# Eight of 22 gated tiles of a down projection as seven block products in place of eight

## The chip, the cores and the metric

One core of a Trainium2 chip runs the kernel. Its engines work side by side, each on a queue of its own that it takes strictly in order: TensorE (PE; PEld is its weight load) multiplies into PSUM, VectorE (DVE) and ScalarE (ACT) do elementwise work, GpSimd (POOL) does some too and issues DMAs, SyncE (SP) only issues DMAs. An instruction that has to wait for another engine or a DMA holds up all that stands behind it on its engine. The metric is the device time of one execution in microseconds (us).

## The reference

A trunk of two layers on a sequence of 1040 positions (16 learned ones and 1024 of input) and 1024 features. Each layer has an attention half, which the change leaves alone, and a feed-forward half:

```python
def conv_ffn(x, w_up, conv_w, conv_b, w_down):
    h = x @ w_up                                  # 1024 -> 2 * 2816
    hc = conv_b + sum(shifted(h, j) * conv_w[j] for j in range(3))
    u, g = jnp.split(hc, 2, axis=-1)
    return (jax.nn.silu(g) * u) @ w_down          # 2816 -> 1024
...
    h = h + conv_ffn(rms_norm(h, ffn_norm[i]), w_up[i], ...)
```

2816 gated features are 22 tiles of 128. The last operation, `@ w_down` and the sum to the residual `h`, is what is changed. All is float32.

## The kernel before, in words

Features lie on the 128 partitions and positions along the free dimension, so that a tile is 128 x 1040 (128 x 1024 in the last layer's down projection, which drops the learned positions). A float32 product is made of three faster ones: each operand is split in a high part, rounded to the type `float32r`, and a low part, the rest. `split` and `weights` do that with a cast on ScalarE (`hi`) and a subtraction on VectorE (`lo`), and `mm3` issues the three matmuls hi·hi, lo·hi, hi·lo (lines 216 to 218).

The up projection (`ffn_up`) makes, for each of the 22 tiles `j`, the two output tiles u and g of 128 features. It does the pair as a 2 x 2 block product with seven block products in place of eight (the scheme of Strassen in Winograd's form): the outputs u and g are the two block rows, the 1024 input features are halved into the inner blocks, and the positions into the two block columns (`HALVES`). Sums of weight blocks (`up_operand`) and of input halves are formed ahead, the seven products p = 1 to 7 are 4 x 2 x 3 matmuls of 260 or 258 columns each, and `evacuate` adds the results out of PSUM. After the last product of a tile, a convolution on ScalarE and VectorE, the gate and a store of the gated tile to DRAM (`actd`) follow. VectorE, ScalarE and the DMA queues are ordered by a planner at build time; TensorE keeps the order of the program.

The down projection then takes the 22 gated tiles in five groups (`FGROUPS`: 5, 5, 5, 4 and 3). `load_act` loads a gated tile (SyncE) and splits it (ScalarE `ah`, VectorE `al`). Within a group and for each of the eight output tiles `m`, `dense3` runs over the group's gated tiles and the chunks of positions (400, 384 and 256 columns in layer 0, 512 and 512 in layer 1), and VectorE adds the sums to the residual tile `hT[m]`, which is in SBUF all that time: it was stored to DRAM (`hm`) in the first half of the layer and is loaded back at the beginning of the down projection. `stream` fetches and splits the weights of one output tile ahead. While the last up tile's seven products run, `during_last` loads ten gated tiles as slots come free; when a group ends its slots take the group after the next. The last three gated tiles (`down_last`) go chunk by chunk, with their weights in slots, so that the next layer's norm can follow.

Buffers: 33 slots of one 128 x 1040 tile, and 6 more in the FFN, are handed out by `Slots.get` and returned by `put`; whoever gets a slot waits for the last reader of its last content. Four 2-bank places of PSUM serve the up projection; the down projection opens a pool of eight single banks.

Of the kernel before, what the change touches and what calls it, by code (L numbers as in the profile page):

```python
# [32 lines left out]
CH_DOWN = [(16, 512), (528, 512)]  # L33
CTILES = [(0, 4), (4, 7), (7, 9)]
FT, NT, FIRST = 116, 9, 112
CH_FOX = [(0, 344), (344, 348), (692, 348)]
# [8 lines left out]
NV = 203  # L45
V_FIN = DEPTH * NV

FGROUPS = [(0, 5), (5, 5), (10, 5), (15, 4), (19, 3)]
HALVES, HALVES_LAST = (0, 520, 520), (8, 524, 516)
AHEAD = 4  # L50
NSPLIT = 4

# [80 lines left out]
class Kern:  # L133
# [843 lines left out]


    def up_operand(self, lyr, j, p, fw, raws, odd):
        nc = self.nc  # L980
        if j == 2 and p in (1, 2):
            src = fw.tile([128, 4, 128], F32, tag="raw2", name="raw2")
            nc.sync.dma_start(src[:], self.wm[lyr, M_UP + 4][:, 4 * p - 4:4 * p, :])
            return self.up_split(src, fw, odd)
        if j not in raws:
            u, g = self.wm[lyr, M_UP + 2 * j], self.wm[lyr, M_UP + 2 * j + 1]
            q = raws[j] = {}
            for name, src, k0, own in (("A11", u, 0, True), ("A21", g, 0, False), ("A22", g, 4, False), ("A12", u, 4, True)):
                q[name] = self.wp.tile([128, 4, 128], F32, tag="raw", name="raw", bufs=4) if own else \
                    fw.tile([128, 4, 128], F32, tag="raw2", name="raw2")  # L990
                nc.sync.dma_start(q[name][:], src[:, k0:k0 + 4, :])
        q = raws[j]

        def combine(out, a, b, op):
            if out not in q:
                q[out] = fw.tile([128, 4, 128], F32, tag="raw2", name="raw2")
            nc.vector.tensor_tensor(out=q[out][:], in0=q[a][:], in1=q[b][:], op=op)
# [8 lines left out]
        return self.up_split(src, fw, odd)  # L1006

    def up_split(self, src, fw, odd):
# [4 lines left out]
        nc.scalar.copy(hi[:], src[:])  # L1013
        nc.vector.tensor_tensor(out=lo[:], in0=src[:], in1=hi[:].bitcast(F32), op=ALU.subtract)  # L1014
        return [(hi[:, k, :], lo[:, k, :]) for k in range(4)]

    def ffn_up(self, lyr, mix, hT, pp, fw, halves, o0, during_last):
        nc, s = self.nc, self.slots
# [218 lines left out]
        s.put(t)  # L1237
        acts[j] = (ah, al)

    def down_tiles(self, lyr, hT, pp, o0, dchunks, acts):  # L1240
        nc, s = self.nc, self.slots

        def down(i, m):
            g0, ng = FGROUPS[i]

            def f(w):
                def ev(ps, c0, n):
                    h = hT[m][:, c0:c0 + n]
                    nc.vector.tensor_tensor(out=h, in0=ps, in1=h, op=ALU.add)
                self.dense3(pp, w, [acts[j] for j in range(g0, g0 + ng)], dchunks, ev)  # L1250
                if m == KD - 1:
                    for j in range(g0, g0 + ng):
                        s.put(*acts.pop(j))
                    if i + 2 < len(FGROUPS):
                        a, b = FGROUPS[i + 2]
                        for j in range(a, a + b):
                            self.load_act(j, o0, acts)
            return (self.wd[lyr, m][:, g0:g0 + ng, :], f)
        return [down(i, m) for i in range(len(FGROUPS) - 1) for m in range(KD)]

    def down_last(self, lyr, hT, pp, dchunks, acts, at_end, es):

        nc, s = self.nc, self.slots
        g0, ng = FGROUPS[-1]
        w, held = [], []
        for m in range(KD):
            if m % 2 == 0:
                pair = [s.get(F32R, "wl", (128, 2, 4, 128), es) for _ in range(2)]
                held += pair
            w.append(self.weights(self.wd[lyr, m][:, g0:g0 + ng, :], [x[:, m % 2, :, :] for x in pair]))  # L1270
        nxt = at_end()
        a = [acts[j] for j in range(g0, g0 + ng)]
        for c0, n in dchunks:
            for m in range(KD):
                ps = pp.tile([128, 512], F32, tag="mm", name="mm")
                for k in range(ng):
                    self.mm3(ps[:, :n], w[m][k], a[k], c0, n, k == 0, k == ng - 1)
                h = hT[m][:, c0:c0 + n]
                nc.vector.tensor_tensor(out=h, in0=ps[:, :n], in1=h, op=ALU.add)
                final = nxt["gain"] is None  # L1280
                if final and c0 + n == T and m >= KD // 2:

                    sq = nxt["tp"].tile([128, 256], F32, tag="sql", name="sql", bufs=4)[:, :n]
                    nc.scalar.activation(sq, h, AF.Square)
                    nxt.setdefault("late", []).append(sq)
                else:
                    self.norm_feed(nxt, m, h, c0, n, nc.vector if final and c0 + n == T else None)
                if not final:
                    nc.sync.dma_start(self.hd[m][:, c0:c0 + n], h)
                elif m == 5 and c0 != dchunks[0][0]:  # L1290
                    self.norm_scale(nxt, pp, *before)
                    if c0 + n < T:
                        self.final(nxt, hT, pp, *before, pool=4)
            if final and c0 + n == T:
                nxt["parts"] = nxt.pop("late")
                self.norm_scale(nxt, pp, c0, n)
                self.final(nxt, hT, pp, *before, pool=KD + 1)
                self.final(nxt, hT, pp, c0, n, pool=KD + 1)
            before = (c0, n)
        for x in a:  # L1300
            s.put(*x)
        s.put(*held)
        return nxt
# [19 lines left out]
    def run(self):  # L1323
# [17 lines left out]
        for lyr in range(DEPTH):  # L1341
# [5 lines left out]
            acts, early = {}, {1: 2, 6: 2, 2: 1, 7: 2, 5: 1, 4: 1, 3: 1}  # L1347

            def during_last(p):
                for _ in range(early[p]):  # L1350
                    self.load_act(len(acts), o0, acts)
            with tc.tile_pool(name=f"ffn{lyr}", bufs=1, reuse_waits="tile") as fp, \
                    tc.manual_schedule(engines={mybir.EngineType.PE}):
                ids = s.add(fp, 6, f"e{lyr}_")
                with tc.tile_pool(name=f"ups{lyr}", bufs=1, space=PSUM, reuse_waits="tile") as pp, \
                        tc.tile_pool(name=f"up{lyr}", bufs=7, reuse_waits="tile") as fw:
                    self.ffn_up(lyr, mix, hT, pp, fw, HALVES_LAST if last else HALVES, o0, during_last)
                with tc.tile_pool(name=f"dps{lyr}", bufs=8, space=PSUM, reuse_waits="tile") as pp, \
                        tc.tile_pool(name=f"down{lyr}", bufs=1, reuse_waits="tile") as dp:
                    ids += s.add(dp, 3 if last else 4, f"d{lyr}_")  # L1360
                    hT = [s.get(F32, f"h{k}", first=ids) for k in range(KD)]
                    for k in range(KD):
                        nc.sync.dma_start(hT[k][:, o0:T], self.hm[k][:, o0:T])
# [9 lines left out]
                    self.stream(self.down_tiles(lyr, hT, pp, o0, CH_DOWN if last else CH, acts))  # L1373
# [60 lines left out]
```

## Time and profile before

| | us |
|---|---|
| median of three runs | 2647.05 (2646.37 to 2649.61) |
| profiled execution | 2645.09 |
| its span, first to last instruction | 2643.3 |
| first four groups of the down projection, layer 0 | 1071.8 to 1288.9 of the span |
| the same, layer 1 | 2380.2 to 2591.5 |

A line of a group reads: line, engine, operation, out<-in, shape, xcount | busy us, mean ns of one | idle time ahead of them and what ended it. A line of the timeline reads: start, duration in us, engine, line, operation, out<-in, shape, xcount, and in brackets the idle time before it and its releaser. The duration of an instruction overlaps a little with the next on the same engine, so that the distance of two starts is its price in a row. A stretch reads: start:end, length, and for each engine its busy us and instruction count, then the granted share of TensorE's clock, the DMA engines' busy share and GB/s.

### The profile page before, as it was taken

How to read it: one execution, taken by the hardware profiler on the slowest of the kernel's cores; microseconds unless marked ns; L12 is line 12 of the kernel's file. 1: busy time of each engine (PE TensorE's matmuls, PEld its weight loads, DVE VectorE, ACT ScalarE, POOL GpSimd, SP SyncE). 2: the span in 40 equal slices, each digit the busy share in tenths (PEclk: the TensorE clock that was granted, in tenths of full speed). 3: DMA queues.
4: the chain of work that ended last, by engine and by line, in shares of the span. 5: the costliest groups of instructions: out<-in, count | busy, mean ns of one | idle time of the engine just before them, and what ended most of it. 6: DMA issues, size and time to landing. Idle time of an engine off the chain costs nothing.

```text
span 2643.3 us, 46336 instructions
## 1 busy us (share of the span) xinstructions
PE 2523.9 (95%) x18102; PEld 2407.2 (91%) x18102; DVE 1759.9 (67%) x3484; ACT 1240.1 (47%) x2677; POOL 457.9 (17%) x596
## 2 busy tenths in 40 slices
PE   8999999897999999999999999998989999999997
PEld 7988898897999999999999888887889999998886
DVE  7655676759877777643665666666698767776335
ACT  6345665645544445421343565665455444453112
POOL 4033333333000000000201333332320000000002
PEclk9999999998999999999999999999999999999999
DMA  3222124341222222632312222142512222245222
GB/s 125 65 83 70 47 83 124 106 131 58 97 81 76 85 77 92 217 94 58 103 56 65 75 72 74 56 138 91 158 51 85 83 81 77 83 139 189 65 55 77
DMA packets 114476, 240.72 MB, mean 91 GB/s; under 512 B 14432, under 2 KB 36192, under 8 KB 114256
## 3 DMA queue, kind: packets, MB, share of 16 engines
q1 hardware_dynamic: 96000, 182.27, 22.7%
q0 software_dynamic: 16384, 53.18, 5.5%
q8 instruction: 142, 2.33, 0.4%
q10 hardware_dynamic: 1872, 2.31, 0.2%
q14 instruction: 78, 0.64, 0.1%
HBM read 174.01 MB, written 50.91 MB: 85 GB/s over the span
## 4 chain that ended last, share of the span: by engine, by line
PE 77%; DVE 13%; ACT 4%; issue 3%; DMA 2%; POOL 2%; DVEq 0%; SPq 0%; POOLq 0%; ACTq 0%
PE mm L216 12%; PE mm L217 12%; PE mm L218 12%; PE up L216 10%; PE up L217 10%; PE up L218 10%; PE av L706 2%; PE tr L688 2%; DVE S L655 1%; DVE x L1038 1%; PE wo L217 1%; PE wo L216 1%; PE wo L218 1%; DVE PT L331 1%; ACT P L667 1%
## 5 line engine op out<-in xcount | busy, mean ns | idle before, releaser
L216 PE MATMUL up<-x,hi 128*128 128x260 f32 (+1 forms) x2464 | 701.3, 285 | 22.7 <-DVE hu L1180 20.3
L217 PE MATMUL up<-x,lo 128*128 128x260 f32 (+1 forms) x2464 | 699.2, 284 | 0.0
L218 PE MATMUL up<-x,hi 128*128 128x260 f32 (+1 forms) x2464 | 698.5, 283 | 0.0
L216 PEld LDWEIGHTS up<-x,hi 128*128 128x128 f32 x2464 | 467.5, 190 | 24.4 <-DVE hu L1180 20.7
L217 PEld LDWEIGHTS up<-x,lo 128*128 128x128 f32 x2464 | 467.9, 190 | 0.1
L218 PEld LDWEIGHTS up<-x,hi 128*128 128x128 f32 x2464 | 467.8, 190 | 0.0
L216 PE MATMUL mm<-xh,hi 128*128 128x348 f32 (+4 forms) x1056 | 365.1, 346 | 0.0
L218 PE MATMUL mm<-xl,hi 128*128 128x348 f32 (+4 forms) x1056 | 340.9, 323 | 0.0
L217 PE MATMUL mm<-xh,lo 128*128 128x348 f32 (+4 forms) x1056 | 340.8, 323 | 0.0
L1014 DVE TENSOR_TENSOR lo<-raw,hi 128x512 fp32r<-128x512 f32 x308 | 212.9, 694 | 146.2 <-ACT hi L1013 146.2
L183 ACT CAST hi<-raw 128x512 fp32r<-128x512 f32 (+1 forms) x264 | 142.3, 543 | 329.8 <-PE mm L218 240.0
L217 PE MATMUL mm<-ah,lo 128*128 128x400 f32 (+1 forms) x760 | 266.4, 351 | 0.2 <-DVE lo L185 0.2
L218 PE MATMUL mm<-al,hi 128*128 128x400 f32 (+1 forms) x760 | 265.9, 350 | 0.0
L216 PE MATMUL mm<-ah,hi 128*128 128x400 f32 (+1 forms) x760 | 265.8, 350 | 0.0
L185 DVE TENSOR_TENSOR lo<-raw,hi 128x512 fp32r<-128x512 f32 (+1 forms) x196 | 120.7, 620 | 181.1 <-ACT hi L183 177.5
L1013 ACT CAST hi<-raw 128x512 fp32r<-128x512 f32 x308 | 190.3, 620 | 107.6 <-PE up L218 92.7
L216 PEld LDWEIGHTS mm<-xh,hi 128*128 128x128 f32 x1056 | 201.0, 190 | 6.0 <-issue 5.3
L217 PEld LDWEIGHTS mm<-xh,lo 128*128 128x128 f32 x1056 | 200.9, 190 | 0.4 <-issue 0.3
L218 PEld LDWEIGHTS mm<-xl,hi 128*128 128x128 f32 x1056 | 199.9, 189 | 0.4 <-issue 0.3
L1203 POOL DMA_DIRECT2D actd<-cv x44 | 23.4, 533 | 830.0 <-DVE cv L1202 830.0
L667 ACT ACTIVATE P<-S,m 116x460 f32<-116x460 f32 (+2 forms) x224 | 124.8, 561 | 76.9 <-DVE m L655 72.6
L331 DVE TENSOR_TENSOR PT<-tr,PT 116x464 fp32r<-116x464 f32 (+3 forms) x240 | 122.1, 516 | 55.8 <-ACT PT L330 54.1
(248 smaller groups left out, 5269.0 us busy)
## 6 DMA issues: line engine op xcount, KB each, us to landing
raw<-in_wm_dram SPq DMA_DIRECT2D x328, 256.0 KB, 2.6
raw<-in_wd_dram SPq DMA_DIRECT2D x64, 256.0 KB, 2.6
actd<-cv POOLq DMA_DIRECT2D x22, 520.0 KB, 2.9
st<-actd SPq DMA_DIRECT2D x22, 520.0 KB, 4.9
actd<-cv POOLq DMA_DIRECT2D x22, 512.0 KB, 3.0
st<-actd SPq DMA_DIRECT2D x22, 512.0 KB, 4.8
cb<-cd SPq DMA_DIRECT2D x16, 520.0 KB, 4.2
kA<-kA SPq DMA_DIRECT2D x24, 260.0 KB, 3.8
```

The costliest lines, as they stand in the source:

```text
L183: nc.scalar.copy(hi[:, :n, :], raw[:, :n, :])
L185: eng.tensor_tensor(out=lo[:, :n, :], in0=raw[:, :n, :], in1=hi[:, :n, :].bitcast(F32), op=ALU.subtract)
L216: nc.tensor.matmul(ps, wh, xh[:, c0:c0 + n], start=first, stop=False, skip_group_check=more)
L217: nc.tensor.matmul(ps, wl, xh[:, c0:c0 + n], start=False, stop=False, skip_group_check=more)
L218: nc.tensor.matmul(ps, wh, xl[:, c0:c0 + n], start=False, stop=last, skip_group_check=more)
L331: nc.vector.tensor_tensor(out=lo, in0=src, in1=hi.bitcast(F32), op=ALU.subtract)
L655: nc.vector.tensor_tensor_reduce(out=S[:rows, :n], in0=S[:rows, :n], in1=cb[:rows, c0:k1], scale=1.0, scalar=(BIG if ci == 0 else m[:rows, ...
L667: nc.scalar.activation(P[:rows, :n], S[:rows, :n], AF.Exp, scale=-1.0, bias=m[:rows, nch - 1:nch], accum_out=(den if nch == 1 else d3[:row ...
L688: nc.tensor.transpose(tr[:w, j, :rows], P[:rows, o:o + w], id_)
L706: nc.tensor.matmul(av[:, a:width], w.rearrange("p a b -> p (a b)"), x, start=(t == 0 and i == 0), stop=(t == last and i == 1))
L1013: nc.scalar.copy(hi[:], src[:])
L1014: nc.vector.tensor_tensor(out=lo[:], in0=src[:], in1=hi[:].bitcast(F32), op=ALU.subtract)
```

## The change

The groups are now one plain group of three gated tiles whose sums leave SBUF ("n"), one block group of eight ("s"), two plain groups of four whose sums are added to the residual in SBUF ("r"), and the last three as before. In the block group a pair of output tiles is the two block rows, the eight gated tiles are two inner halves of four, and the positions the two block columns: seven block products for a pair in place of eight, with weight sums made by the same function as in the up projection (`block_operand`, split off `up_operand`).

The operands of the block group, seven sums or differences of gated tiles, each split in hi and lo, are made by the new generator `prepare`. It yields how many slots its next step needs, and `pump` lets it go on when so many are free: after each product of the last up tile, after each plain tile and after each block product. Sums of the plain "n" group and of the block group are copied or added out of PSUM into a slot and added to the residual in DRAM (`hm`) by DMAs that accumulate, eight for each of the two groups and layer, on the GpSimd queue. Only then is the residual loaded (`load_residual`). All plain tiles work on the two halves of positions in two pieces, so on 260 or 256 columns, and use the four 2-bank places of the up projection, in whose pools the stage now runs.

```diff
-FGROUPS = [(0, 5), (5, 5), (10, 5), (15, 4), (19, 3)]
+GROUPS, LAST = (("n", 0, 3), ("s", 3, 8), ("r", 11, 4), ("r", 15, 4)), (19, 3)
+HALVES, HALVES_LAST, HALVES_OUT = (0, 520, 520), (8, 524, 516), (16, 528, 512)
...
+    def prepare(self, halves, acts, X):
...
+        for kind, g0, ng in GROUPS + (("r",) + LAST,):
+            if kind != "s":
+                for j in range(g0, g0 + ng):
+                    yield 3
+                    self.load_act(j, halves[0], acts)
+                continue
...
+            for k0 in range(0, nk, 2):
...
+                a0, a1 = load(g0, 0), load(g0, 1)
+                put(1, a0)
+                yield 2 + m
+                b0, b1 = load(g0 + nk, 0), load(g0 + nk, 1)
+                put(2, b0)
+                yield 1 + m
+                tt(a1, b1, a1, ALU.subtract)
+                t2 = get("t2")
+                tt(t2, a1, a0, ALU.add)
+                put(6, t2)
+                yield m
+                tt(a0, b1, t2, ALU.subtract)
+                put(5, a0)
...
+    def pump(self, keep):
+        s = self.slots
+        while self.need + keep <= len([i for i in s.free if i not in s.lent]):
+            self.need = next(self.prep)
...
+    def down_blocks(self, lyr, g0, ng, X, pp, fw, halves, first):
...
+        for j in range(NP):
+            seq += [(j, 2), (j, 6), (j, 5), (j, 7)] + ([(j + 1, 1)] if j + 1 < NP else []) + [(j, 4), (j, 3)]
...
+            elif p == 4:
+                copy(q["g"][:, t0])
+                nc.gpsimd.dma_start(self.hm[2 * j + 1][:, o0:T], q["g"][:, o0:T], accum_op=ALU.add)
+                s.put(q["g"])
+            elif p == 3:
+                add(q["u"][:, t1], q["x"])
+                nc.gpsimd.dma_start(self.hm[2 * j][:, o0:T], q["u"][:, o0:T], accum_op=ALU.add)
+                s.put(q["u"])
...
+    def ffn_down(self, lyr, pp, fw, halves, acts, X, ids):
...
+        def load_residual():
+            for k in range(KD):
+                hT.append(s.get(F32, f"h{k}", first=ids))
+                nc.sync.dma_start(hT[k][:, o0:T], self.hm[k][:, o0:T])
...
+                if kind == "n":
+                    nc.gpsimd.dma_start(self.hm[m][:, o0:T], out[:, o0:T], accum_op=ALU.add)
+                    s.put(out)
...
-                    self.ffn_up(lyr, mix, hT, pp, fw, HALVES_LAST if last else HALVES, o0, during_last)
+                    self.ffn_up(lyr, mix, hT, pp, fw, HALVES_LAST if last else HALVES, o0, lambda p: self.pump(3))
+                    hT = self.ffn_down(lyr, pp, fw, halves, acts, X, ids)
```

More of the change, by code (lines that the diff above doesn't have):

```diff
@@ L996, in combine @@
                 q[out] = fw.tile([128, 4, 128], F32, tag="raw2", name="raw2")
-            nc.vector.tensor_tensor(out=q[out][:], in0=q[a][:], in1=q[b][:], op=op)
+            nc.vector.tensor_tensor(out=q[out][:, :nk, :], in0=q[a][:, :nk, :], in1=q[b][:, :nk, :], op=op)
         if p == 6:
@@ L1012, in up_split @@
         lo = pool.tile([128, 4, 128], F32R, tag="lo" + x, name="lo", bufs=3)
-        nc.scalar.copy(hi[:], src[:])
-        nc.vector.tensor_tensor(out=lo[:], in0=src[:], in1=hi[:].bitcast(F32), op=ALU.subtract)
-        return [(hi[:, k, :], lo[:, k, :]) for k in range(4)]
+        nc.scalar.copy(hi[:, :nk, :], src[:, :nk, :])
+        nc.vector.tensor_tensor(out=lo[:, :nk, :], in0=src[:, :nk, :], in1=hi[:, :nk, :].bitcast(F32), op=ALU.subtract)
+        return [(hi[:, k, :], lo[:, k, :]) for k in range(nk)]
     def ffn_up(self, lyr, mix, hT, pp, fw, halves, o0, during_last):
@@ new lines, in pump, with ensure, evacuate @@
+    def pump(self, keep):
[3 more added lines that the diff above has]
+    def down_blocks(self, lyr, g0, ng, X, pp, fw, halves, first):
+        nc, s = self.nc, self.slots
+        nk, o0, W = ng // 2, halves[0], halves[2]
+        n = W // 2
+        t0, t1 = (slice(c, c + W) for c in halves[:2])
+        two = lambda ap: ap.rearrange("p (a b) -> p a b", b=n)
+        NP = KD // 2
+        seq = [(0, 1)]
+        for j in range(NP):
+            seq += [(j, 2), (j, 6), (j, 5), (j, 7)] + ([(j + 1, 1)] if j + 1 < NP else []) + [(j, 4), (j, 3)]
+        raws, ops, st = {}, [], {}
+        wd = lambda m: self.wd[lyr, m][:, g0:g0 + ng, :]
+        def ensure(i):
+            while len(ops) < min(i + AHEAD + 1, len(seq)):
+                j, p = seq[len(ops)]
+                ops.append(self.block_operand(wd(2 * j), wd(2 * j + 1), nk, j, p, fw, raws, len(ops) % 2))
+        def evacuate(j, p):
+            q = st[j]
+            add = lambda out, ps: nc.vector.tensor_tensor(out=two(out), in0=ps[:, :, :n], in1=two(out), op=ALU.add)
+            copy = lambda out: nc.scalar.copy(two(out), q["a"][:, :, :n])
+            if p == 1:
+                q["u"] = s.get(F32, "du")
+                copy(q["u"][:, t0])
+            elif p == 2:
+                add(q["u"][:, t0], q["y"])
+            elif p == 6:
+                copy(q["u"][:, t1])
+            elif p == 7:
+                q["g"] = s.get(F32, "dg")
+                copy(q["g"][:, t1])
+                add(q["g"][:, t1], q["x"])
+            elif p == 4:
[6 more added lines that the diff above has]
+                s.put(q["u"])
+                del st[j]
+        ensure(0)
+        first()
+        for i, (j, p) in enumerate(seq):
+            ensure(i)
+            q = st.setdefault(j, {})
+            bank, begins = {2: "y", 5: "x", 3: "x"}.get(p, "a"), p in (1, 2, 5)
+            if begins:
+                place = {1: j % 2, 2: 3, 5: 2}[p]
+                q[bank] = pp.tile([128, 2, 512], F32, tag=f"p{place}", name="down", bufs=1)
+            ps, w = q[bank], ops[i]
+            ops[i] = None
+            for k in range(nk):
+                _, hi, lo = X[p][k // 2]
+                for c in range(2):
+                    self.mm3(ps[:, c, :n], w[k], (hi[:, k % 2, :], lo[:, k % 2, :]), c * n, n,
+                             begins and k == 0, k == nk - 1, not begins)
+            evacuate(j, p)
+            if j == NP - 1:
+                for held, _, _ in X.pop(p):
+                    s.put(*held)
+            self.pump(4)
@@ L1253, in f @@
                         s.put(*acts.pop(j))
[L1254 to L1257, printed above, removed]
+                self.pump(3)
             return (self.wd[lyr, m][:, g0:g0 + ng, :], f)
-        return [down(i, m) for i in range(len(FGROUPS) - 1) for m in range(KD)]
+        i = 0
+        while i < len(GROUPS):
+            kind, g0, ng = GROUPS[i]
+            i += 1
+            if kind == "r":
+                if not hT:
+                    load_residual()
+                tiles = [plain(kind, g0, ng, m) for m in range(KD)]
+                while i < len(GROUPS) and GROUPS[i][0] == "r":
+                    tiles += [plain(*GROUPS[i], m) for m in range(KD)]
+                    i += 1
+                self.stream(tiles)
+            elif kind == "n":
+                tiles = [plain(kind, g0, ng, m) for m in range(KD)]
+                if i < len(GROUPS) and GROUPS[i][0] == "s":
+                    self.stream(tiles[:-1])
+                    w = self.weights(tiles[-1][0])
+                    _, a, b = GROUPS[i]
+                    i += 1
+                    self.down_blocks(lyr, a, b, X[a], pp, fw, halves, lambda: tiles[-1][1](w))
+                else:
+                    self.stream(tiles)
+        if not hT:
+            load_residual()
+        while any(j not in acts for j in range(LAST[0], sum(LAST))):
+            self.need = next(self.prep)
+        return hT
     def down_last(self, lyr, hT, pp, dchunks, acts, at_end, es):
         nc, s = self.nc, self.slots
-        g0, ng = FGROUPS[-1]
+        g0, ng = LAST
         w, held = [], []
@@ L1346, in run @@
             dch = CH_OUT if last else CH
[L1347 to L1351, printed above, removed]
+            acts, X = {}, {}
+            halves = HALVES_OUT if last else HALVES
+            self.prep = self.prepare(halves, acts, X)
+            self.need = next(self.prep)
             with tc.tile_pool(name=f"ffn{lyr}", bufs=1, reuse_waits="tile") as fp, \
@@ L1360, in run @@
                     ids += s.add(dp, 3 if last else 4, f"d{lyr}_")
-                    hT = [s.get(F32, f"h{k}", first=ids) for k in range(KD)]
-                    for k in range(KD):
-                        nc.sync.dma_start(hT[k][:, o0:T], self.hm[k][:, o0:T])
                     def at_end():
```

75 lines of the change are left out of this document (58 added, 17 removed).

## The prediction

> **What bounds the kernel now.** I read the page first, then the stretches of the stage that is changed, then the instructions around its beginning.
>
> ```profile
> span 2643.3 us, 46336 instructions
> PE 2523.9 (95%) x18102; PEld 2407.2 (91%) x18102; DVE 1759.9 (67%) x3484; ACT 1240.1 (47%) x2677; POOL 457.9 (17%) x596
> PE 77%; DVE 13%; ACT 4%; issue 3%; DMA 2%; POOL 2%; DVEq 0%; SPq 0%; POOLq 0%; ACTq 0%
> ```
>
> TensorE (PE) carries 77% of the chain that ended last, so the kernel is bound by its matmuls and what matters is each moment in which TensorE has to wait. The stretches (us, then busy time and count per engine, granted clock, DMA share, GB/s):
>
> ```profile
> 1071.80:1288.90 217.10, 216.87 (x1370) 216.56 (x1369) 98.59 (x181) 49.15 (x82) 0.53 (x1) 1.00 0.33 102
> 2380.20:2591.50 211.30, 211.30 (x915) 171.60 (x914) 96.29 (x147) 47.98 (x80) 0.53 (x1) 1.00 0.32 98
> 2326.00:2366.00 40.00, 40.00 (x335) 40.00 (x335) 30.64 (x38) 22.67 (x33) 1.06 (x2) 1.00 0.32 96
> 1936.20:1946.40 10.20, 0.16 (x2) 0.06 (x1) 9.03 (x12) 6.11 (x11) 4.38 (x3) 0.74 0.00 0
> 1946.40:1951.60 5.20, 5.20 (x25) 5.20 (x26) 4.71 (x8) 1.14 (x2) 0.00 (x0) 0.52 0.28 102
> 1952.00:1960.00 8.00, 8.00 (x69) 8.00 (x68) 8.00 (x9) 3.27 (x6) 4.84 (x3) 1.00 0.06 23
> ```
>
> The first two rows are the first four groups of the down projection (19 gated tiles) in layer 0 and layer 1: TensorE never stops in them, VectorE (DVE, third pair of numbers) is busy 45% and the DMA engines 33%. So fewer matmul columns save time there one for one, as long as nothing makes TensorE wait. The third row is the up projection's block products in layer 1: 335 matmuls of 258 columns in 40 us, 0.12 us each. The other three rows are used below. The beginning of the stage, TensorE in layer 0:
>
> ```profile
> 1071.52 0.28 PE L217 MATMUL up<-x,lo 128*128 128x260 f32 x1
> 1071.64 0.28 PE L218 MATMUL up<-x,hi 128*128 128x260 f32 x1
> 1071.76 0.34 PE L216 MATMUL mm<-ah,hi 128*128 128x400 f32 x1
> 1072.34 0.45 PE L217 MATMUL mm<-ah,lo 128*128 128x400 f32 x1 [0.23 <-DVE lo L185]
> ```
>
> The last up matmul and the first down matmul follow at 0.12 us, and the second waits 0.23 us for `lo`, the low part of the first down weight, which VectorE makes. This hand-over is free now because of where that one instruction stands in VectorE's queue:
>
> ```profile
> 1055.12 0.69 DVE L1180 TENSOR_TENSOR hu<-up,hu 128x520 f32<-128x520 f32 x1
> 1055.73 1.29 DVE L1173 SCALAR_TENSOR_TENSOR cv<-hg,vec,cv 128x1038 f32<-128x1038 f32 x1
> 1056.94 1.24 DVE L331 TENSOR_TENSOR al<-st,ah 128x1040 fp32r<-128x1040 f32 x1
> 1058.09 1.30 DVE L1173 SCALAR_TENSOR_TENSOR cv<-hu,vec,cv 128x1039 f32<-128x1039 f32 x1
> 1059.31 0.68 DVE L1014 TENSOR_TENSOR lo<-raw,hi 128x512 fp32r<-128x512 f32 x1
> 1059.91 1.29 DVE L1173 SCALAR_TENSOR_TENSOR cv<-hu,vec,cv 128x1038 f32<-128x1038 f32 x1
> 1061.12 1.23 DVE L331 TENSOR_TENSOR al<-st,ah 128x1040 fp32r<-128x1040 f32 x1
> 1062.27 1.23 DVE L1202 TENSOR_TENSOR cv<-cv 128x1040 f32<-128x1040 f32 x1
> 1071.60 0.69 DVE L185 TENSOR_TENSOR lo<-raw,hi 128x512 fp32r<-128x512 f32 x1
> 1072.20 2.39 DVE L331 TENSOR_TENSOR al<-st,ah 128x1040 fp32r<-128x1040 f32 x2
> 1075.31 0.69 DVE L1180 TENSOR_TENSOR hu<-up,hu 128x520 f32<-128x520 f32 x1
> ```
>
> The weight's `lo` (1071.60) stands ahead of the final sum of the last up tile (1075.31). The starts also give VectorE's price per instruction in a row: 0.61 us for a 520-wide sum (1055.12 to 1055.73), 1.21 for a convolution step, 1.15 for a 1040-wide split or sum (1061.12 to 1062.27), 0.60 for a 512-wide `lo`.
>
> **The change, part by part.**
>
> *TensorE's work.* Layer 0's 19 tiles are now 19·8·3·3 = 1368 matmuls in 217.1 us. Afterwards 11 tiles stay plain at 11·8·3·4 = 1056 matmuls of 260 columns, and 8 tiles become 28 block products of 24 matmuls, 672: together 1728. At 0.12 us: 207.4, 9.7 saved. Layer 1's 912 matmuls of 512 columns take 211.3 us, 0.2317 each; the 1728 of 256 columns at 0.12·256/260 = 0.1182 take 204.2, 7.1 saved. Sum −16.8. The Trainium skill (Perfetto Trace Analysis, Optimizing Tensor Performance) says that larger matmuls are more efficient than smaller ones, which speaks against cutting 512 into 256: if width were free, layer 1 would save 211.3/19 = 11.1 in place of 7.1; the trace bears the page out by 2% a column (2·0.1182 against 0.2317).
>
> *The hand-over from up to down.* This decides. In the changed program the block operands of tiles 3 to 10 (`prepare`) are made while the last up tile runs, and VectorE's queue is written in this order, from the final sum of up tile 20 (the row at 1055.12) on:
>
> ```
> sum hu, conv, split x1, conv, lo, conv, diff, u*g of tile 20, t2, sum hg, diff,
> split x6, x7, x2, x5, diff, split x3, sum hu, split x4,
> sum hu (waits for the last up product),
> split x1, conv, split x2, conv, conv, conv, diff, u*g of tile 21, t2, split x3, diff,
> split x6, diff, split x5, x7, x4, lo of the first down weight
> ```
>
> That is 4 sums (4·0.61 = 2.4), 7 convolution steps (7·1.21 = 8.5), 14 splits, 8 block sums and 2 products 1040 wide (24·1.15 = 27.6), one 512-wide `lo` (0.6) and one 384-wide:
>
> ```profile
> L185 DVE TENSOR_TENSOR wl<-raw,wl 128x384 fp32r<-128x384 f32 x16 | 8.7, 557 | 18.0 <-ACT wl L183 17.8 <-PE mm L218 0.3
> L330 ACT CAST ah<-st 128x1040 fp32r<-128x1040 f32 x22 | 23.4, 1063 | 27.8 <-DMA st<-actd 25.8 <-DVE al L331 1.8
> L1181 ACT COPY hu<-up 128x520 f32<-128x520 f32 x44 | 26.1, 592 | 67.3 <-PE up L218 67.3
> 1063.80 0.53 POOL L1203 DMA_DIRECT2D actd<-cv  x1 [20.77 <-DVE cv L1202]
> ```
>
> 0.56 us, in all 39.7 us. The loads and stores of the stage (KB each, us from issue to landing):
>
> ```profile
> raw<-in_wd_dram SPq DMA_DIRECT2D x64, 256.0 KB, 2.6
> actd<-cv POOLq DMA_DIRECT2D x22, 520.0 KB, 2.9
> st<-actd SPq DMA_DIRECT2D x22, 520.0 KB, 4.9
> h<-hm SPq DMA_DIRECT2D x8, 520.0 KB, 8.5
> ```
>
> Before, the row at 1055.12 starts 16.6 us ahead of the first down matmul. So `lo` is there 39.7 − 16.6 = 23.1 us after TensorE's last up matmul, and TensorE, which does its matmuls in order, stands at the second matmul of the stage until then. The list cannot begin earlier than the up product that its first sum reads, 6·24·0.12 = 17.3 us before the end: the floor is 22.4. Upward: split x2 waits for a load that is issued only when split x3 has freed the slot, then for ScalarE's cast (1.06 us); a half load of 2.6 to 4.9 us, its issue and the cast against 3.6 us of VectorE's other work add 0.6 to 3. I take 23.9 in layer 0 and, 1024 wide, 23.3 in layer 1: +47.2. What hides the same splits before is that TensorE already has plain tiles to work on; here the eight tiles' operands are prepared ahead of three plain tiles' first weight, so the cover comes after the work.
>
> *TensorE's clock after such a stop.* The rows 1936.2 to 1960 show it at the start of layer 1's FFN:
>
> ```profile
> 1936.02 0.28 PE L218 MATMUL up<-x,hi 128*128 128x258 f32 x1
> 1946.34 0.58 PE L216 MATMUL up<-x,hi 128*128 128x258 f32 x1 [10.04 <-DVE hu L1180]
> ```
>
> After 10 us idle TensorE runs at a granted clock of 0.52 for 5.2 us, in which it does 25 matmuls in place of 5.2/0.12 = 43: 5.2 − 25·0.12 = 2.2 us lost. Twice: +4.4. The Trainium skill (TensorE: Matmul & The Clock Gate, Part 1) has the clock halved after an idle window of about 3.4 us and released after one busy window as long; by that an estimate is 1.7 a stop, 3.4 in the sum. The row is longer than the page's window.
>
> *The plain group (3 tiles).* Its operands are ready when TensorE resumes; a tile is 36 matmuls, 4.3 us, with two `lo` or less and two ScalarE copies behind it: nothing. Its eight sums go to the residual in DRAM by an accumulating DMA of 520 KB on the GpSimd queue, eight more follow from the block products. No row of the profile is such a DMA. The nearest is the store `actd<-cv`: a plain store from the same queue lands in 2.9 us; with a read of the same bytes in front of it 2.9 + 4.9 = 7.8. I call this L and take 4, nearer to the store, the only row of the same queue and direction.
>
> *The block products.* Per pair of output tiles VectorE has 4 weight sums, 7 `lo` (0.60) and 3 sums, 8.5 us, against 7·24·0.12 = 20.2 on TensorE; no stop from load. What waits for an accumulating DMA is a slot that it read from. (a) VectorE's split of tile 11 waits for the sixth plain sum to land, and the `lo` of the second block product of the stage stands behind it: covered by the two remaining plain tiles and two products until L is about 6; at 7.8 it costs 3.5 a layer. (b) In the last pair the load of tile 16 waits for an accumulate that is issued 1.8 us ahead of the pair (a product of 2.88 less the copy, 0.59, and the issue, 0.53), and ScalarE's copy (0.59) that frees the bank of the fourth product stands behind that tile's cast: there −1.8 + L + 4.9 + 1.06 + 0.59 = 4.8 + L into the pair, needed at 3·2.88 = 8.6. Five more casts ahead of the next copy delay that too. Together 1.4 at L = 2.9, about 2 at L = 4, 6.2 at 7.8. I take +4.0 for both layers, with 2.8 and 2·(6.2 + 3.5) = 19.4 as ends.
>
> *Reloading the residual.* The eight loads of `h`, issued before at the hand-over, now stand in SyncE's queue in the last pair, h7 and h6 behind the last two accumulates. The loads start some 5.8 us before the block stage ends and the first lands 8.5 us later; two plain tiles of 48 matmuls (11.5 us) run before TensorE needs the banks back. The weights of three tiles are fetched ahead of the blocked loads, the fourth are needed 17 us after the stage and their load waits for h7's accumulate, 1.1 + L after the last product but one. Hidden up to L of about 14; without that cover each us of L would count.
>
> *The last group.* Its matmuls are those of before, 400 wide in the first chunk, 0.18 us from start to start:
>
> ```profile
> 1281.80 0.34 PE L216 MATMUL mm<-ah,hi 128*128 128x400 f32 x1
> 1281.98 0.35 PE L217 MATMUL mm<-ah,lo 128*128 128x400 f32 x1
> ```
>
> Two of four pairs of its weights find slots only when the last plain tile releases them; two rounds of a load (2.6), a cast and a `lo` (0.56, the 384-wide row) are through in some 8 us, and the last weights are needed after six of the group's products, 6·9·0.18 = 9.8: nothing.
>
> Sum against the profiled execution (2645.1 us, span 2643.3): −16.8 + 47.2 + 4.4 + 4.0 = +38.8, 2683.9. The median of the runs, 2647.05, is 2.0 above it: 2686.
>
> **The rivals.** (1) As forecast: slower by TensorE's wait for `lo` at both hand-overs, 2672 to 2698. (2) The accumulating DMAs take over 7 us, and (a) and (b) come on top: at 7.8, 2686 − 4 + 19.4 = 2701, and some 4 us per us of L beyond. For it: nothing in the trace bounds the read-modify-write. Against: the DMA engines are a third busy in the stage. (3) The other side: VectorE's queue at the hand-over doesn't stop TensorE, and the matmuls saved come through, 2647 − 17 = 2630. It needs the wait to fall under 16.8/2 − 2.2 = 6.2 us a layer; VectorE would have to run the 39.7 us in 23, against every row above. (4) The block products don't come cheaper, since VectorE or the banks stop TensorE in them as the up stage is stopped at times: 2686 + 17 = 2703 at worst. (5) Within 0.2%, by the stop and the saving cancelling at 8 us a layer: no row speaks for it.
>
> **How the numbers follow.** 0.2% is 5.3 us, about what a measurement of this kernel tells from no change. Chances: (1) 0.80, (2) 0.11, (4) 0.03, (5) 0.03, (3) 0.03. So faster 0.03, same 0.03, slower 0.94. The range is 2672 to 2708: below, the floor of 22.4 and 22 a hand-over, no cost in the last pair, and 3 us a layer if the list starts or runs somewhat better; above, 3 us more a hand-over, L = 7.8 and a little of (4).
>
> **What would show it.** In the changed kernel's TensorE rows: one gap of 21 to 28 us in each layer behind the first down matmul, released by VectorE's `lo`, and 5 us at a clock of about 0.5 behind it. 1728 matmuls at 0.12 us in each stage. Small gaps of 1 to 3 us in the last pair of block products, released by ScalarE's copies. Accumulating DMAs landing in 3 to 6 us, and no gap when the residual comes back. Wrong it would be if `lo` came before TensorE needs it, if the accumulates took 8 us and more, or if the gap after the block products were the larger.

## The result, and the profile after

The changed kernel takes 2726.4 us (median of four runs, 2724.3 to 2732.4) against 2646.7 (2644.5 to 2649.6): 1.0304 times as long, 95% interval 1.0284 to 1.0324. The forecast was 2686 with a range of 2672 to 2708. The direction and the largest term were right, but half of the loss was not foreseen.

From the page of the changed kernel, its span, engines, DMA queues and the chain that ended last (shares of the span):

```profile
span 2726.0 us, 48785 instructions
PE 2528.9 (93%) x19278; PEld 2448.7 (90%) x19278; DVE 1796.7 (66%) x3464; ACT 1289.9 (47%) x2745; POOL 485.9 (18%) x628
...
q0 software_dynamic: 20992, 70.09, 8.9%
...
PE 43%; issue 33%; DVE 13%; ACT 4%; DMA 3%; POOL 3%; SPq 0%; DVEq 0%; POOLq 0%; ACTq 0%
```

TensorE's busy time, in which a matmul at a slow clock counts in full, grew by 5 us only, the span by 82.7: the rest is waiting. The stage in both layers (1728 matmuls each), and the 5 us behind its first stop:

```profile
1070.50:1326.50 256.00, 215.92 (x1730) 214.45 (x1729) 110.20 (x145) 69.75 (x108) 14.38 (x17) 0.92 0.44 115
2423.40:2673.10 249.70, 211.06 (x1730) 209.62 (x1729) 108.93 (x145) 68.91 (x107) 14.36 (x17) 0.93 0.44 116
1095.10:1100.10 5.00, 5.00 (x23) 5.00 (x24) 0.84 (x2) 0.59 (x1) 0.00 (x0) 0.50 0.38 118
```

256.0 and 249.7 us stand against 217.1 and 211.3 before. Below, a stop is counted as the distance of two matmuls' starts less the usual distance (0.12 us in layer 0, 0.118 in layer 1), and what a part of the stage lost as its length less the usual distance for each of its matmuls. Without all that was lost the two stages would be 207.4 and 203.9 us, so the saving of 17 us was there. What was lost:

| us lost on TensorE | forecast, a layer | layer 0 | layer 1 |
|---|---|---|---|
| hand-over from up to down | 23.9 / 23.3 | 24.4 | 23.7 |
| slow clock behind it | 2.2 | 2.5 | 2.4 |
| last two tiles of the plain group | 0 | 2.4 | 3.1 |
| third block product, with slow clock | 0 | 9.7 | 9.4 |
| middle of the block group, with slow clock | 0 | 4.0 | 1.3 |
| last pair of block products, with slow clock | 2 | 5.7 | 6.1 |
| reload of the residual, last group | 0 | 0 | 0 |

Outside the two stages another 5 us came, between them. That stretch before and after:

```profile
1288.90:2380.20 1091.30, 1040.95 (x7906) 1006.44 (x7905) 768.91 (x1560) 561.81 (x1241) 217.68 (x285) 0.99 0.28 88
1326.50:2423.40 1096.90, 1048.50 (x7907) 1013.71 (x7905) 776.20 (x1570) 566.43 (x1252) 218.13 (x285) 0.98 0.28 89
```

TensorE does the same matmuls there and waits no longer than before (1096.9 less 1048.5 us against 1091.3 less 1041.0), but is busy 7.6 us longer, at a granted clock of 0.98 in place of 0.99. So this loss is clock, not waiting. The hand-over, on TensorE and on VectorE:

```profile
1070.38 0.28 PE L219 MATMUL up<-x,hi 128*128 128x260 f32 x1
1070.51 0.28 PE L217 MATMUL down<-ah,hi 128*128 128x260 f32 x1
1095.06 0.59 PE L218 MATMUL down<-ah,lo 128*128 128x260 f32 x1 [24.27 <-DVE lo L186]
```

```profile
1068.80 2.39 DVE L332 TENSOR_TENSOR x<-st,x 128x1040 fp32r<-128x1040 f32 x2 [1.10 <-ACT x L331]
...
1090.99 3.54 DVE L332 TENSOR_TENSOR x<-st,x 128x1040 fp32r<-128x1040 f32 x3
1094.45 1.49 DVE L186 TENSOR_TENSOR lo<-raw,hi 128x384 fp32r<-128x384 f32 x3
```

The second down matmul waits 24.27 us for the first weight's `lo`, and that stands directly behind the last three splits of block operands. From 1054.1 to there VectorE runs the list of the prediction in its order, with one wait of 1.10 us, ahead of the split of x2. Then the stop that was not forecast, at the third block product, in order of time over GpSimd, VectorE, SyncE, ScalarE and TensorE:

```profile
1130.63 1.06 ACT L331 CAST ah<-st 128x1040 fp32r<-128x1040 f32 x1 [2.98 <-DMA st<-actd]
1131.60 0.58 ACT L1401 COPY do<-down 128x520 f32<-128x520 f32 x1
...
1132.48 0.86 POOL L1403 DMA_DIRECT2D hm<-do  x1 [9.29 <-ACT do L1401]
...
1138.19 1.24 DVE L332 TENSOR_TENSOR al<-st,ah 128x1040 fp32r<-128x1040 f32 x1 [4.77 <-DMA hm<-do]
1139.35 1.29 DVE L1018 TENSOR_TENSOR lo<-raw,hi 128x512 fp32r<-128x512 f32 x2
...
1140.50 2.12 SPq L1238 DMA_DIRECT2D st<-actd  x2
...
1146.76 1.06 ACT L331 CAST ah<-st 128x1040 fp32r<-128x1040 f32 x1 [10.95 <-DMA st<-actd]
1147.72 0.58 ACT L1333 COPY du<-down 128x520 f32<-128x520 f32 x1
...
1148.36 0.58 PE L217 MATMUL down<-x,hi 128*128 128x260 f32 x1 [7.95 <-ACT du L1333]
```

The first two rows belong to the stop ahead of this one, in the last plain tile: the copy `do` that TensorE needs stands behind a cast that waited 2.98 us for its load. Then an accumulating DMA, that of the sixth plain sum, is issued at 1132.48 and lands at 1138.2. VectorE's split of a gated tile waits for it, since it writes the slot that the DMA reads; behind the split stands a weight's `lo`, and on SyncE a weight's load waits for that `lo`. Only behind this load SyncE issues the next gated tiles' loads, at 1140.50, and the first lands at 1146.7. ScalarE's cast of it waits, and behind the cast stands the copy `du` out of the PSUM bank that the third product goes on adding to. In the last pair it is the same engine and the same kind of instruction:

```profile
1219.99 1.06 ACT L331 CAST ah<-st 128x1040 fp32r<-128x1040 f32 x1 [4.76 <-DMA st<-actd]
1220.96 0.58 ACT L1333 COPY du<-down 128x520 f32<-128x520 f32 x1
```

The DMA issues of the changed kernel (KB each, median us to landing):

```profile
raw<-in_wd_dram SPq DMA_DIRECT2D x64, 256.0 KB, 4.1
st<-actd SPq DMA_DIRECT2D x14, 520.0 KB, 5.3
hm<-do POOLq DMA_DIRECT2D x8, 520.0 KB, 6.8
h<-hm SPq DMA_DIRECT2D x8, 520.0 KB, 4.5
hm<-dg POOLq DMA_DIRECT2D x4, 520.0 KB, 6.2
hm<-du POOLq DMA_DIRECT2D x4, 520.0 KB, 6.4
```

The accumulating DMAs land after 6.2 to 6.8 us in layer 0 (5.4 to 6.4 in layer 1, at 512 KB), and the down weights, which landed in 2.6 before, take 4.1.

### The profile page after: what moved, and what is told of

The parts are those of the page before. It is cut to its first block, busy times and chain, and to the rows that moved or that the text cites. A ratio compares the mean times of both kernels' runs of the same rounds, so it can differ in the third digit from the quotient of the medians.

```text
span 2726.0 us, 48785 instructions
## 1 busy us (share of the span) xinstructions
PE 2528.9 (93%) x19278; PEld 2448.7 (90%) x19278; DVE 1796.7 (66%) x3464; ACT 1289.9 (47%) x2745; POOL 485.9 (18%) x628
## 4 chain that ended last, share of the span: by engine, by line
PE 43%; issue 33%; DVE 13%; ACT 4%; DMA 3%; POOL 3%; SPq 0%; DVEq 0%; POOLq 0%; ACTq 0%
PE mm L217 6%; PE mm L219 6%; PE mm L218 6%; PE down L217 4%; PE down L218 4%; PE down L219 4%; PE av L707 2%; PE tr L689 2%; DVE S L656 2%; PE up L217 1%; PE up L218 1%; DMA st<-actd 1%; PE up L219 1%; DVE x L1042 1%; DVE PT L332 1%
## 5 line engine op out<-in xcount | busy, mean ns | idle before, releaser
L1018 DVE TENSOR_TENSOR lo<-raw,hi 128x512 fp32r<-128x512 f32 x364 | 251.4, 693 | 200.1 <-ACT hi L1017 200.1
L1017 ACT CAST hi<-raw 128x512 fp32r<-128x512 f32 x364 | 225.0, 620 | 154.2 <-PE up L219 93.4
L218 PE MATMUL down<-ah,lo 128*128 128x260 f32 (+1 forms) x704 | 200.8, 285 | 48.1 <-DVE lo L186 48.1
L184 ACT CAST hi<-raw 128x512 fp32r<-128x512 f32 (+2 forms) x200 | 116.7, 587 | 208.2 <-PE down L219 96.8
L217 PE MATMUL down<-ah,hi 128*128 128x260 f32 (+1 forms) x704 | 200.5, 285 | 4.1 <-ACT do L1401 4.1
L219 PE MATMUL down<-al,hi 128*128 128x260 f32 (+1 forms) x704 | 200.1, 284 | 0.0
L218 PEld LDWEIGHTS down<-ah,lo 128*128 128x128 f32 x704 | 134.8, 191 | 48.7 <-DVE lo L186 48.7
## 6 DMA issues: line engine op xcount, KB each, us to landing
raw<-in_wm_dram SPq DMA_DIRECT2D x328, 256.0 KB, 2.8
raw<-in_wd_dram SPq DMA_DIRECT2D x64, 256.0 KB, 4.1
```

The source lines that it names most:

```text
L184: nc.scalar.copy(hi[:, :n, :], raw[:, :n, :])
L217: nc.tensor.matmul(ps, wh, xh[:, c0:c0 + n], start=first, stop=False, skip_group_check=more)
L218: nc.tensor.matmul(ps, wl, xh[:, c0:c0 + n], start=False, stop=False, skip_group_check=more)
L219: nc.tensor.matmul(ps, wh, xl[:, c0:c0 + n], start=False, stop=last, skip_group_check=more)
L1017: nc.scalar.copy(hi[:, :nk, :], src[:, :nk, :])
L1018: nc.vector.tensor_tensor(out=lo[:, :nk, :], in0=src[:, :nk, :], in1=hi[:, :nk, :].bitcast(F32), op=ALU.subtract)
```

## The experiments

Five of the seven kernels ran once. The kernel before, run beside them, spread from 2642.2 to 2651.7 us, so a difference of a few us is read from the stops in the traces and not from the times.

### Plain stores in place of accumulating DMAs

The sums to the residual are left out here; the tiles are stored over it.

```diff
-nc.gpsimd.dma_start(self.hm[m][:, o0:T], out[:, o0:T], accum_op=ALU.add)
+nc.gpsimd.dma_start(self.hm[m][:, o0:T], out[:, o0:T])
```

and the same in the block group.

> Of the changed kernel, with its 16 accumulating DMAs a layer replaced by plain stores of the same tiles from the same queue (the sum to the residual is left out). The trace of the changed kernel shows a TensorE stop of 24.4 and 23.7 us at the hand-over (layer 0, layer 1), one of 8.1 and 7.6 us at the third block product, and two of together 4.1 and 4.4 in the last pair. Theory A (the stop at the third product is a chain that begins where an accumulate lands: landing, split on VectorE, issue of a load on SyncE, the load, cast on ScalarE, copy that frees the bank): landing falls from 6.5 to about 3 us, the stop at the third product shrinks by the same 3 to 4 us to about 4 and does not go, the last pair's fall to about 2 together, the hand-over stays at 24: about 2710 us (2704 to 2716). Theory B (the accumulates slow all loads by what they move): the stop at the third product goes wholly, loads of weights fall from 4.1 back to 2.6 us: about 2698. Theory C (the accumulates have no part in it, the order alone has): 2726, nothing moves.

Measured: 2699.3 us, 27 less. The stop at the third product fell from 8.1 and 7.6 to 2.4 and 0.4 us, those ahead of it and in the middle of the block group went, the last pair's fell to 1.5 and 1.9, with 1.6 of slow clock behind the third product in layer 0 and behind the last pair in layer 1; the hand-over did not shrink (26.3 and 24.7).

```profile
q0 software_dynamic: 20992, 70.09, 7.0%
raw<-in_wd_dram SPq DMA_DIRECT2D x64, 256.0 KB, 3.0
hm<-do POOLq DMA_DIRECT2D x8, 520.0 KB, 3.9
hm<-du POOLq DMA_DIRECT2D x4, 520.0 KB, 4.0
```

So the accumulates cost 27 us in all, nearly as theory B has it: more goes than the shorter landing explains, and the weights' loads are faster too. It doesn't yet say whether a wait for a landing or slower loads did it.

### Slots of their own for the accumulated tiles

```diff
+self.own = Slots()
+self.own.free = [i for i in s.free if i not in s.lent][:4]
+s.drop(self.own.free)
...
-q["u"] = s.get(F32, "du")
+q["u"] = self.own.get(F32, "du")
```

Likewise for `dg` and `do`, and `pump` keeps no further slots. No load or split of a gated tile waits for an accumulate now.

> The changed kernel with four slots kept for the tiles that the accumulating DMAs read, so that no load of a gated tile waits for an accumulate; the DMAs are as they were. Theory A: landing stays at 6 to 7 us, the stop at the third block product falls from 8.1 and 7.6 us to 0 to 2, the one of 1.7 and 2.2 ahead of it goes, the last pair's 4.1 and 4.4 fall to 0 to 3; hand-over unchanged at 24.4 and 23.7: about 2698 us (2690 to 2706). Theories B and C: the stop at the third product stays within 2 us of what it was, 2715 to 2726.

Measured: 2715.6 us. The stops in the middle of the block group went, and those ahead of the block group fell to 0.6 and 0.7; but the one at the third product stayed at 6.6 and 8.2 us. My theory A missed: with the wait for the landing gone, the load itself is late. On SyncE, ScalarE and TensorE, and the DMA engines from 1132 to 1146 us:

```profile
1133.03 1.17 SPq L1238 DMA_DIRECT2D st<-actd  x2
...
1144.43 1.06 ACT L331 CAST ah<-st 128x1040 fp32r<-128x1040 f32 x1 [9.43 <-DMA st<-actd]
1145.39 0.58 ACT L1333 COPY du<-down 128x520 f32<-128x520 f32 x1
...
1146.03 0.58 PE L217 MATMUL down<-x,hi 128*128 128x260 f32 x1 [6.45 <-ACT du L1333]
```

```profile
q0 software_dynamic: 415, 1.53, 55.4%
q1 hardware_dynamic: 862, 2.11, 41.4%
...
st<-actd SPq DMA_DIRECT2D x2, 520.0 KB, 11.6
hm<-do POOLq DMA_DIRECT2D x1, 520.0 KB, 8.9
```

The load is issued 7.5 us earlier than in the changed kernel (1133.03), and takes 11.6 us (median of the two), where the median in the changed kernel is 5.3 and the same two loads beside plain stores took 6.3. The 16 DMA engines are 97% busy in these 14 us, and the accumulates' queue (q0) holds 55% of their time while it moves 1.53 of 3.65 MB. The Trainium skill (DMA: Bandwidth & Descriptors, Queues, rings and completion order) says that a DMA engine takes turns between the queues that have work, a packet at a time; by that a load's packets each wait for one of an accumulate. The row of 11.6 us fits that, but no run here shows the order of the packets.

### The loads of gated tiles held back as well

Until the sixth block product is copied out, with own slots kept. GpSimd writes eight columns of three slots behind that copy, and `prepare`, which stands still until then, loads gated tiles 11 to 13 into these slots:

```diff
+def gate(src):
+    ids = [i for i in s.free if i not in s.lent][-3:]
+    for i in ids:
+        t = s.get(F32, "gate", first=[i])
+        nc.gpsimd.tensor_tensor(out=t[:, o0:o0 + 8], in0=src[:, o0:o0 + 8], in1=src[:, o0:o0 + 8], op=ALU.add)
+        s.put(t)
+    self.gated = ids
+    self.need = next(self.prep)
...
+if i == 5:
+    gate(st[seq[i][0]]["u"])
```

> The kernel with the four own slots, and besides the loads of gated tiles 11 to 13 held back until the sixth block product is copied out (GpSimd writes eight columns of their slots after it), so that no cast of a late tile stands on ScalarE ahead of the copies that free the banks of the first products. The accumulating DMAs stay. If the stop at the third block product (6.6 and 8.2 us with own slots) is ScalarE's copy behind a cast whose load is slow beside the accumulates, it goes to under 1 us in both layers, and the 1 us of slow clock behind it: 2715.6 - 17 = 2699 (2695 to 2704). If the weights of the block products are what is late under that traffic, 3 us or more a layer stay, released by VectorE or ScalarE for the weights: 2705 to 2716. The hand-over stays at 24, the last pair at 2.6 and 3.7.

Measured: 2699.4 us, as expected to half a us, and as much as plain stores gave. Both stops at the third product are gone, though the accumulates land as late as ever. The stretch around it in layer 0, and the DMA issues in that stretch:

```profile
1130.00:1150.00 20.00, 20.00 (x168) 19.89 (x167) 8.27 (x14) 8.81 (x16) 2.58 (x3) 1.00 0.74 167
```

```profile
hm<-do POOLq DMA_DIRECT2D x3, 520.0 KB, 8.5
raw<-in_wd_dram SPq DMA_DIRECT2D x6, 256.0 KB, 6.0
```

TensorE runs through the 20 us without a gap, with weights that take 6 us and accumulates that take 8.5. So neither is the cause by itself: it is the cast of a late tile ahead of the copy of a bank on ScalarE.

### Block operands made later

`yield 99` asks for more slots than there are, so `prepare` stands still there until the fifth plain tile moves it on.

```diff
+            yield 99
             nk = ng // 2
...
+                if kind == "n" and m == 4:
+                    self.need = next(self.prep)
```

> The changed kernel with the block operands begun only when the fifth of the eight plain tiles is issued in the program, in place of at the hand-over; so the first three down weights stand ahead of most of them in VectorE's queue. If the hand-over's stop is VectorE's queue ahead of the first weight's low part, both stops (24.4 and 23.7 us) and the 2 us of slow clock behind each go: 2726 - 52 = 2674. VectorE then has 28 us of block operands to make within some 36 us of plain tiles, so that up to 6 us a layer may come back at the weights of the fourth to eighth tile or at the first block products: 2674 to 2686. If the stop was the weight's load or cast, or if VectorE can't make the operands beside the plain tiles, it comes back at full size: over 2700.

Measured: 2675.5 us, 1.5 above the lower of the two figures. The stop at the hand-over is gone in both layers:

```profile
1076.05 0.28 PE L219 MATMUL up<-x,hi 128*128 128x260 f32 x1
1076.17 0.28 PE L217 MATMUL down<-ah,hi 128*128 128x260 f32 x1
1076.28 0.28 PE L218 MATMUL down<-ah,lo 128*128 128x260 f32 x1
```

The plain group loses 8.0 and 5.0 us now, in small stops, where its end lost 2.4 and 3.1; the block group loses 13.1 and 12.8, where it lost 19.4 and 16.7. The one about makes up for the other, so that the time comes out so near 2674 is in part luck; that the stop is gone is not.

### Both, and then room for the operands

The later operands and the own slots together:

> Both of the last two edits together. If the two causes are separate and complete, their gains add: 2726 - 52 - 28 = 2646, with 2638 to 2656 for what may come back; with all stops gone it would be 2647 - 17 = 2630 and the 5 us that the changed kernel lost outside the down projection. If they are one cause (VectorE's queue in both), the gains don't add and it stays over 2665.

Measured: 2663.5 us (2660.6 to 2664.5, 1.0057 times the kernel before, 1.0035 to 1.0078). This lies between the two outcomes that were put down, 2638 to 2656 and over 2665. The measured gains do add: 50.9 us from the later operands and 10.8 from the own slots make 61.7, and 62.9 came. The 2646 had counted 28 for the own slots, which they had not given. The plain group still loses 9.0 and 10.6 us, and the last pair 4.5 and 5.5. The plain group is 35 us long without its stops, and VectorE and ScalarE have 37 and 28 us of work in it (third and fourth pair), with operand loads of 4.7 to 7.8 us between the steps:

```profile
1072.70:1116.20 43.50, 36.88 (x291) 36.26 (x290) 37.00 (x41) 28.49 (x42) 6.66 (x8) 0.96 0.72 168
```

So a fourth gated tile went into the plain group:

```diff
-GROUPS, LAST = (("n", 0, 3), ("s", 3, 8), ("r", 11, 4), ("r", 15, 4)), (19, 3)
+GROUPS, LAST = (("n", 0, 4), ("s", 4, 8), ("r", 12, 4), ("r", 16, 3)), (19, 3)
```

with three own slots in place of four.

> Hold and own slots together (2663.5), with four gated tiles in the plain group in place of three (groups of 4, 8, 4, 3 and 3; three own slots), so that the block operands are made beside 46 us of plain matmuls in place of 35. If the 9.0 and 10.6 us that TensorE still loses in the plain group are VectorE's and ScalarE's work on the operands, they fall to under 3 us a layer: 2663.5 - 14 = 2649 (2643 to 2655). If they are slow loads (the operands' halves land late beside the accumulates, whatever the time there is), they stay over 6 us a layer: 2657 to 2666.

Measured: 2645.9 us. The plain group loses nothing now:

```profile
1072.80:1118.80 46.00, 46.00 (x386) 46.00 (x385) 36.50 (x40) 28.57 (x40) 6.62 (x8) 1.00 0.77 183
2377.00:2422.60 45.60, 45.59 (x386) 45.38 (x385) 36.00 (x40) 27.96 (x40) 6.68 (x8) 1.00 0.69 166
```

VectorE has 36.5 us of work in 46. The longer group gives the loads more time as well, so how much of the stops was work and how much late loads is not shown. The time is not told apart from the kernel before (2643.5 to 2651.2). What is left is 4.2 us at the third product in layer 1, and two stops of 2.1 to 3.0 and 0.8 to 0.9 us in each last pair, with the slow clock behind them. The last kernel holds back the loads there too, as above, and a second time until the last block product is copied out, with the groups ("r", 12, 3) and ("r", 15, 4) behind the block group.

> The last two edits together with a second hold: the tiles after the first plain group behind the block group are loaded only after the last block product is copied out (groups 4, 8, 3, 4 and 3). With every cause found so far taken away, the plain group loses under 3 us a layer, the third product nothing and the last pair (2.9 and 3.9 with 1.5 of slow clock, released by ScalarE behind late casts) under 1: 2663.5 - 14 - 3 - 10 = 2636 (2630 to 2645), under the kernel before (2648). If the last pair's stop is the accumulates' own or the weights', it stays and 2646 comes out; if tiles that come that late stop the plain groups behind the block group, up to 10 us a layer come there.

Measured: 2636.7 us (median of nine, 2633.2 to 2641.7), 0.9962 times the kernel before, 95% interval 0.9952 to 0.9973: faster than the changed kernel and, by a little, than the kernel before.

```profile
1068.10:1277.80 209.70, 207.84 (x1730) 207.24 (x1729) 112.38 (x151) 75.09 (x116) 15.53 (x23) 1.00 0.57 150
2372.10:2578.70 206.60, 205.02 (x1731) 204.34 (x1731) 111.60 (x149) 73.55 (x114) 15.58 (x23) 1.00 0.54 144
```

```profile
hm<-do POOLq DMA_DIRECT2D x8, 520.0 KB, 5.6
hm<-du POOLq DMA_DIRECT2D x4, 520.0 KB, 6.6
```

The two stages lose 2.4 and 2.6 us, and the clock is granted in full. With the same block products and the same 16 accumulates a layer, landing after 5.6 to 6.6 us (5.7 to 6.9 in layer 1), the two stages now take 12.1 us less than the kernel before.

## Why the prediction was wrong

**TensorE's work: right.** 17.1 us saved where 16.8 was forecast; a 256-wide matmul cost 0.118 us. The last kernel brings most of it home.

**The hand-over: right in place, releaser and size.** 24.4 and 23.7 us against 23.9 and 23.3, from counting what stood in VectorE's queue ahead of `lo`. The list ran as counted, and its one wait came where 0.6 to 3 us were put down. The later operands prove the cause: with `lo` ahead of them the stop is gone.

**The slow clock: right.** 23 matmuls in the first 5.0 us at a granted clock of 0.50, 2.2 us lost in them and 2.5 and 2.4 in all, where 2.2 was put down. The estimate by the Trainium skill (TensorE: Matmul & The Clock Gate, Part 1), 1.7, stays below the row here too.

**The accumulating DMA: this step failed.** Its price was too low: "L and take 4, nearer to the store" measured 5.4 to 6.8, nearer to the upper end of 7.8, which stood in the range. (The store that it went by was not the only row of that queue and direction, but the other, `hm<-h` of 260 KB, landed in 2.6 us before and would not have warned.) But the price is the smaller part. By the prediction's own paths, an L of 6.5 would give about 1 us for (a), between 0 at 6 and 3.5 at 7.8, and about 5 for (b), between 2 and 6.2: in all some 8 us more than was taken, so 2694. What failed is the path. The text let an accumulate act only through the slot that it reads, and followed that through VectorE's queue to the second block product. The wait that (a) names was there, and that DMA landed in 5.7 us, under the 6 at which (a) costs nothing; the second product was not stopped. Yet the end of the plain group and the third product lost 12.1 and 12.5 us, which had been put at nothing. Two things were left out. First, from VectorE the wait goes on over SyncE's queue to the next gated tile's load, and ScalarE's cast of that tile stands ahead of the copy of the first product's bank; I had not followed SyncE's and ScalarE's queues there. Holding back these loads took the stop away. Second, an accumulate takes time on the DMA engines, so that loads which wait for nothing land late (11.6 us): with the waits taken away, the stop stayed. Rival (2) had the accumulates as the cause, but asked for an L of over 7, which the medians did not reach, and went by the same two paths, so its 2701 is far too small.

**The last pair: right mechanism, too small.** ScalarE's copies behind the casts of late tiles, as (b) says, but 5.7 and 6.1 us in place of 2: L was longer, two copies came late (1.5 and 2.6 us in layer 0), and 1.5 of slow clock behind them was not counted. In the last kernel, which holds those loads back, 0.9 us is left.

**Block products and residual: nearly right.** The products came at 0.12 us a matmul; "no stop from load" failed in the middle of the group (4.0 and 1.3), again through a slot of an accumulate, since own slots removed it. The residual's loads and the last group cost nothing, as forecast.

**Outside the stage.** The work between the two stages took 1096.9 us against 1091.3, a term that the prediction did not have. It is the same work in all these kernels, and took 1090.0 us (operands later, own slots) to 1096.6 (own slots and held loads) in the others, at a granted clock of 0.99 and 0.98. So the clock makes the difference; why it falls more often in some of them was not settled.

In sum the stages lost 94.5 us where 55.6 was forecast; of the 38.9 between, nearly all lies in the plain group's end and the block group, and plain stores gave back 27 of it.

## What to carry to other kernels

Where an engine takes its queue in order, list what stands ahead of the instruction that empties a bank as carefully as what stands ahead of an operand: here a cast that waited for a load held up a copy of 0.58 us, and TensorE with it for 8. Price a new kind of DMA both as a latency and as time on the DMA engines that other loads then lack. And before giving up an idea whose work was saved but lost again in waiting, look for cover: the same block products went from 3.0% slower to 0.4% faster by moving work behind matmuls that can hide it and by keeping back loads that nobody needed yet.

## What the runs showed of the hardware

- An accumulating DMA costs over twice the DMA engines' time of a plain store. The rows of GpSimd's queue (q0) give 5.5% of 16 engines before, 8.9% after and 7.0% with plain stores, for the same 4608 packets added. If the queue's other packets took as long as before, that is (0.089·2726.0 − 0.055·2643.3)·16/4608 = 0.34 us a packet, against (0.070·2697.6 − 0.055·2643.3)·16/4608 = 0.15.
- Its issue held GpSimd for 0.86 us, where the plain store of the same tile took 0.53.
- A load of 520 KB that landed in 4.9 us before took 11.6 beside accumulates, with the engines 97% busy, and 6.3 beside plain stores.
- The clock fell behind short stops too: in the middle of the block group a stop of 2.40 us (layer 0) was followed by 1.6 us lost at a slow clock, one of 1.25 us at the same place (layer 1) by none.
